# Padding the SBUF pools of a hybrid decoder step so that the operands of its large products begin at multiples of 256 bytes

## The chip, the core and the metric

The kernel runs on one core of a Trainium2 chip. The metric is the device time of one execution in microseconds, as the median of several. The profile is taken by the hardware profiler from one further execution.

## The reference

One inference step of a one-layer decoder, for a prompt of 2048 new tokens and for 8 sampled sequences of 8 new tokens with 8192 cached positions each. All data are float32. Cut to what matters:

```python
z = x @ w_in                                   # 1024 -> 3600 columns
fox = softmax(q k^T / 8 + L_i - L_j, causal) v # 8 heads of 64, forget gates as a bias
C, n, m, h = mlstm_scan(q, k, v, i, f)         # 4 heads of 128, matrix memory
mix = concat(fox, norm(h) * gate) @ w_o
x1  = layer_norm(ALPHA * x + mix)
hid = square(relu(x1 @ w1))                    # 1024 -> 4096
y   = layer_norm(ALPHA * x1 + hid @ w2)        # 4096 -> 1024
```

For the samples the attention also runs over pages of a key and value cache, which a page table points to.

## The kernel before

**Large products.** `mm3` (L152 to L155) makes each float32 product out of three single-pass products of a rounded high part and a low part: high by high (L153), low by high (L154), high by low (L155). `split_hi` on ScalarE (L145) writes the high part, `split_lo` on VectorE (L148) the low one. In `T.matmul(out, a, b)` the program loads `a` as the stationary operand and streams `b` past it. In the groups of the profile the streamed (moving) operand comes first: `ph<-x1h,wh 128*128 128x512` stands for a product into `ph` that streams 512 columns of `x1h` past 128 columns of `wh`. Each moving row of 512 float32 is 2048 contiguous bytes of a partition, and each stationary operand of 128 columns is 512 bytes.

**Stages.** Block A (`block_a`, called for four blocks of tokens) computes the input projection into PSUM tiles `pm`, with 256, 272 or 320 moving columns, and feeds the mLSTM recurrence (`m_block`, `m_sample`). Phase B (`phase_b`) does the prompt's attention, head by head: scores `pS` from `ks` and `qh`/`ql`, softmax, transposes `pt` of `S` into `PT`, and `po` from `vn` and `PT`. Phase O (`phase_o`) is the output projection `pw` from `wh`/`wl`, `woh`/`wol` and `mh`/`ml`, with the first layer norm. Phase C (`phase_c`) is the MLP: `ph` from `x1h`/`x1l` and the pieces `wh`/`wl` of w1, squared relu into `hh`/`hl`, and `py` from these and w2, added into `y`. In its last block 576 tokens are streamed as two pieces of 288 columns. The attention of the samples (`sample_attention`) is a generator that `tick` and `attend` advance in between: it gathers cache pages into `kT` and `vt` by indirect transfers and computes `sQ`, `sT` and `sO` in plain float32.

**Order.** The code gives a priority order; a planner at compile time lays out each engine's queue from it and inserts the waits. [...] Transfers are issued from the SP queue, and the gathers from GpSimd (POOL).

**SBUF.** Tiles are taken from pools. Left of the middle stand `cst` (L58) and then `pa` for block A, `pb` for phase B, or `pc` followed by `po` or `ph` for phases O and C. On the right stand `ps` (L85) for the samples, and below it `pm` or `pcw`, `pk`, `py`, `pob` and `px`. A pool's tiles follow one another in the order of their first use, each rounded to 32 bytes. A pool opened where an older one was reuses its bytes, and the first instruction on a new tile waits until the tiles that stood there are done with (`reuse_waits="tile"`). The constants `jp`, `ident`, `nhalf` and `gbias` make `cst` 1120 bytes long, so that what follows it does not begin at a multiple of 256.

The tiles that hold operands: `xn`, `wra`, `whi`, `wlo`, `xh0`, `xl0`, `xh1`, `xl1`, and `kT`, in `pa`; `kn`, `qn`, `qh`, `vn`, `ql`, `nl`, `ks`, `S`, `PT` in `pb`; `wh`, `wl` in `pc`; `mh`, `ml` in `po`; `hh`, `hl` in `ph`; `woh`, `wol` in `pob`; `x1h`, `x1l` in `px`; `wr`, `xr` in `pcw`; `PTs`, `vt` and `S` in `ps`.

Of the kernel before, what the change touches and what calls it, by code (L numbers as in the profile page):

```python
# [10 lines left out]
F32 = mybir.dt.float32  # L11
# [41 lines left out]
def body(ctx, tc, I, O, stages):  # L53
    nc = tc.nc
    V, A, G, T, SY = nc.vector, nc.scalar, nc.gpsimd, nc.tensor, nc.sync


    cst = ctx.enter_context(tc.tile_pool(name="cst", bufs=1))  # L58
# [20 lines left out]
    nhalf = cst.tile([128, 8], F32, name="nhalf")  # L79
    V.memset(nhalf, -0.5)  # L80
    gbias = cst.tile([128, 16], F32, name="gbias")


    es_s = ExitStack()
    ps_ = es_s.enter_context(tc.tile_pool(name="ps", bufs=1, side="right", reuse_waits="tile"))  # L85
# [101 lines left out]
    pa = es_a.enter_context(tc.tile_pool(name="pa", bufs=1, reuse_waits="tile"))  # L187
# [29 lines left out]
    V.memset(rm8.rearrange("p (c t) -> p c t", t=8)[:, :, 0], 0.0)  # L217
    Lend = pa.tile([8, 1], F32, name="Lend")
    mend = pa.tile([4, 1], F32, name="mend")

    head = [0, None]

# [595 lines left out]
    for bi in range(4):  # L818
        g = block_a(bi)
# [21 lines left out]
    def phase_b():  # L841
        es = ExitStack()
        pb = es.enter_context(tc.tile_pool(name="pb", bufs=1, reuse_waits="tile"))
# [94 lines left out]

        def values(z, g, sc):

            for i, (st, mx) in enumerate(sc):
                qt = 2 * g + i
                n = (qt + 1) * 128
                lp = pb.tile([128, 4], F32, name="lp", bufs=6)
                for k, sp in enumerate(st):
                    w = min(512, n - k * 512)
                    last["ACT"] = A.activation(sp[:, :w], sp[:, :w], AF.Exp, bias=mx[:, 7:8], accum_out=lp[:, k:k + 1])
                V.tensor_reduce(z["ls"][:, qt:qt + 1], lp[:, :len(st)], axis=AX.X, op=OP.add)

            po = ppb.tile([128, 256], F32, name="po", bufs=1)  # L950
            nk = 2 * g + 2
            for k0 in range(0, nk, 4):
                PT = pb.tile([128, 4, 256], F32, name="PT", bufs=4)
                for i in range(2):
                    kk = min(4, 2 * g + i + 1 - k0)
                    if kk <= 0:
                        continue
                    pt = ppb.tile([128, 4, 128], F32, name="pt", bufs=3)
                    for k in range(kk):
                        T.transpose(pt[:, k], sc[i][0][k0 // 4][:, k * 128:(k + 1) * 128], ident)  # L960
                    dst = PT[:, :kk, i * 128:i * 128 + 128]
                    if i == 0 or (k0 // 4) % 2 != 0:
                        A.copy(dst, pt[:, :kk])
                    else:
                        V.tensor_copy(dst, pt[:, :kk])
                for k in range(k0, min(k0 + 4, nk)):
                    q0 = 128 if k == nk - 1 else 0
                    c = (k % 2) * 64
                    last["PE"] = T.matmul(po[c:c + 64, q0:], z["vn"][:, k], PT[:, k - k0, q0:],
                                          start=(k < 2), stop=(k >= nk - 2), skip_group_check=True)  # L970
                tick(0.45 * min(4, nk - k0))
            if g % 4 == 0:
                z["ot"] = pb.tile([64, 1024], F32, name="ot", bufs=2)
            od = z["ot"][:, (g % 4) * 256:(g % 4) * 256 + 256]
            A.copy(od, po[0:64])
            q0 = 128 if g == 0 else 0
            V.tensor_tensor(od[:, q0:], od[:, q0:], po[64:128, q0:], op=OP.add)
            if g % 4 == 3:
                finish(z, g // 4)
# [23 lines left out]
        queries(Z[0], 0)  # L1003
        Z[0].update(head(0))
        dmask = masks[0]
        V.memset(dmask, 0.0)
        G.affine_select(dmask, dmask, pattern=[[-1, 128]], compare_op=OP.is_ge, fill=NEG, base=0, channel_multiplier=1)
        keys(Z[0], 0, kn)
# [2 lines left out]
        for n in range(len(units) + LA):  # L1011
# [4 lines left out]
            if n < len(units):  # L1016
                h, g = units[n]
# [11 lines left out]
            if n >= LA:  # L1029
                h, g = units[n - LA]  # L1030
# [71 lines left out]
    def phase_o(halves):  # L1102
        C["py"] = es_c.enter_context(tc.tile_pool(name="py", bufs=1, side="right", reuse_waits="tile"))
        C["pc"] = pc = es_c.enter_context(tc.tile_pool(name="pc", bufs=1, reuse_waits="tile"))
        es, es_b, es_x = ExitStack(), ExitStack(), ExitStack()
        po_ = es.enter_context(tc.tile_pool(name="po", bufs=1, reuse_waits="tile"))
        pob = es_b.enter_context(tc.tile_pool(name="pob", bufs=1, side="right", reuse_waits="tile"))
        ppo = es.enter_context(tc.tile_pool(name="ppo", bufs=1, space=PSUM, reuse_waits="tile"))

        def mix(t, eng):  # L1110
            mr = landing().rearrange("p (k c) -> p k c", k=8)
            SY.dma_start(mr, dmv[:, :, t * 128:(t + 1) * 128])
            mh = po_.tile([128, 8, 128], F32R, name="mh", bufs=2)
            ml = po_.tile([128, 8, 128], F32R, name="ml", bufs=2)
            split_hi(mh, mr)
            split_lo(ml, mr, mh, eng)
            return mh, ml

        vx["more"] = lambda: pob.tile([128, 1024], F32, name="vx", bufs=2)
        wh, wl = [[], []], [[], []]  # L1120

        def weights(hf):
            for q in range(4):
                r = halves.pop(0) if halves else half_wo(hf, q)
                if hf == 0:
                    h, l = piece(None, r)
                    if q == 0:
                        V.memset(pc.tile([128, 512], F32, name="hq", bufs=1)[:, 0:1], 0.0)
                else:
                    h = pob.tile([128, 2, 512], F32R, name="woh", bufs=4)  # L1130
                    l = pob.tile([128, 2, 512], F32R, name="wol", bufs=4)
                    split_hi(h, r)
                    split_lo(l, r, h)
                wh[hf] += [h[:, 0], h[:, 1]]
                wl[hf] += [l[:, 0], l[:, 1]]

        m, xs = {}, {}

        def begin(t):
            xs[t] = row()  # L1140
            SY.dma_start(xs[t], x_of(t))

        def unit(t, hf):
            s = slice(hf * 512, (hf + 1) * 512)
            ps = ppo.tile([128, 512], F32, name="pw", bufs=4)
            for k in range(8):
                mm3(ps, m[t][0][:, k], m[t][1][:, k], wh[hf][k], wl[hf][k], k == 0, k == 7)
            V.scalar_tensor_tensor(xs[t][:, s], xs[t][:, s], ALPHA, ps, op0=OP.mult, op1=OP.add)
            tick(5.1)

        def end(t):
            layer_norm(xs[t], 128, *gb, pc, "1")
            SY.dma_start(dx1[t * 128:(t + 1) * 128], xs[t])

        m[0] = mix(0, None)
        weights(0)
        m[1] = mix(1, None)
        begin(0)
        begin(1)
        unit(0, 0)  # L1160
        weights(1)
        unit(1, 0)
        gb = [bcast(I[f"ln1_{x}"], 0, D, f"{x}1", pcw, tag="wr", bufs=4) for x in "gb"]
        unit(0, 1)
        m[2] = mix(2, G)
        end(0)
        unit(1, 1)
        end(1)
        for t in range(2, 14):
            if t == 13:  # L1170
                vx["more"] = None
            m[t + 1] = mix(t + 1, G)
            begin(t)
            unit(t, 0)
            unit(t, 1)
            end(t)

        m[15] = mix(15, G)
        begin(14)
        begin(15)  # L1180
        nx = [x1_load(0), x1_load(1)]
        unit(14, 1)
        take_back()
        unit(15, 1)
        es_b.close()
        C["px"] = es_c.enter_context(tc.tile_pool(name="px", bufs=1, side="right", reuse_waits="tile"))
        ppx = es_x.enter_context(tc.tile_pool(name="ppx", bufs=1, space=PSUM, side="right", reuse_waits="tile"))
        px_of = lambda: ppx.tile([128, 4, 128], F32, name="px", bufs=2)
        x1_turn(0, 0, nx[0], px_of)
        nx.append(x1_load(2))  # L1190
        unit(14, 0)
        x1_turn(1, 1, nx[1], px_of)
        nx.append(x1_load(3))
        end(14)
        unit(15, 0)
        x1_turn(2, 2, nx[2], px_of)
        x1_turn(3, 3, nx[3], px_of)
        C["w1"] = w1_pieces(0)
        end(15)
        es_x.close()  # L1200
        es.close()
# [129 lines left out]
def sample_attention(tc, I, O, ps_, pps, cst, ident, dnl, dR, dmix, dqb, vx, kx, pa):  # L1331
# [46 lines left out]
    G.affine_select(tri, tri, pattern=[[-1, 128]], compare_op=OP.is_gt, fill=0.0, base=0, channel_multiplier=1)  # L1378
    V.memset(tri[64:128, 0:64], 0.0)
    onesr = ps_.tile([128, 1], F32, name="onesr")  # L1380
    V.memset(onesr, 1.0)
    LG = []
    for g in range(4):
# [2 lines left out]
    for g in range(4):  # L1386
        yield 1
        lv = LG[g].rearrange("p (t h) -> p t h", h=8)
        ri = pa.tile([128, 8, 129], F32, name="ri", tag="kT", bufs=1)
        V.memset(ri[:, :, 128], 0.0)  # L1390
        for h in range(8):
# [349 lines left out]
```

## Time and profile before

| | |
|---|---|
| median of 3 runs | 3387.81 us (3377.21 to 3388.4) |
| the profiled execution, its own time | 3392.21 us |
| its span, first to last instruction | 3390.5 us |
| mean granted TensorE clock | 0.985 |
| block A and the recurrence | to about 920 us |
| phase B | about 925 to 1370 us |
| phase O | about 1370 to 1600 us |
| phase C | about 1600 us to the end |

In the profile, PE is TensorE's matmuls and PEld its loads of stationary operands, DVE is VectorE, ACT ScalarE, POOL GpSimd. A group's row reads: line, engine, operation, output and inputs, stationary shape, moving shape, count, then busy microseconds, mean nanoseconds of one, and the idle time just before them with what ended it. A row of the timeline reads: start in microseconds, duration, engine, line, operation. Matmuls overlap, so that the time of one is read from start to start. A row of the waits gives the total, the number and the longest. In a row of stretches the columns are the stretch, its length, busy time of each engine with the number of instructions, granted clock, share of the DMA engines and GB/s.

### The profile page before, as it was taken

How to read it: one execution, taken by the hardware profiler on the slowest of the kernel's cores; microseconds unless marked ns; L12 is line 12 of the kernel's file. 1: busy time of each engine (PE TensorE's matmuls, PEld its weight loads, DVE VectorE, ACT ScalarE, POOL GpSimd, SP SyncE). 2: the span in 40 equal slices, each digit the busy share in tenths (PEclk: the TensorE clock that was granted, in tenths of full speed). 3: DMA queues.
4: the chain of work that ended last, by engine and by line, in shares of the span. 5: the costliest groups of instructions: out<-in, count | busy, mean ns of one | idle time of the engine just before them, and what ended most of it. 6: DMA issues, size and time to landing. Idle time of an engine off the chain costs nothing.

```text
span 3390.5 us, 58224 instructions
## 1 busy us (share of the span) xinstructions
PE 3263.4 (96%) x22065; PEld 2642.0 (78%) x22065; DVE 1884.5 (56%) x4774; ACT 1361.9 (40%) x2795; POOL 870.8 (26%) x925
## 2 busy tenths in 40 slices
PE   8999998999889999999999999999999999999998
PEld 8998998888756667676777777777776777888886
DVE  6847474464388887434444455445554445644545
ACT  4333343333278888313332333233333423433332
POOL 0131242323322222475223324323252110100000
PEclk9999999999999999999999999999999999999999
DMA  5575766766662322687777768667588444432221
GB/s 180 156 217 187 223 216 231 244 225 218 204 167 83 92 84 52 238 289 243 283 239 241 246 231 292 249 215 273 208 291 278 171 167 147 162 122 81 87 75 66
DMA packets 316001, 650.48 MB, mean 192 GB/s; under 512 B 61001, under 2 KB 175049, under 8 KB 314825
## 3 DMA queue, kind: packets, MB, share of 16 engines
q1 hardware_dynamic: 239032, 367.55, 35.4%
q0 software_dynamic: 74304, 270.57, 22.1%
q10 hardware_dynamic: 2384, 8.65, 0.7%
q8 instruction: 174, 2.85, 0.4%
q14 instruction: 107, 0.87, 0.1%
HBM read 593.82 MB, written 52.83 MB: 191 GB/s over the span
## 4 chain that ended last, share of the span: by engine, by line
PE 48%; DMA 3%; DVE 2%; issue 1%; ACT 1%; POOL 1%; another core or an unknown queue 0%; SPq 0%; POOLq 0%; ACTq 0%; DVEq 0%
PE py L153 7%; PE py L155 7%; PE py L154 7%; PE ph L153 7%; PE ph L155 7%; PE ph L154 7%; PE sO L1598 3%; PE sQ L1486 2%; DMA wr<-w 2%; PE sT L1555 1%; DVE wl L148 1%; PE pw L154 0%; PE pw L155 0%; PE pw L153 0%
## 5 line engine op out<-in xcount | busy, mean ns | idle before, releaser
L1292 DVE TENSOR_TENSOR y<-y,py 128x512 f32<-128x512 f32 (+1 forms) x476 | 324.1, 685 | 420.9 <-PE py L155 337.0
L145 ACT ACTIVATE wh<-wr 128x1024 fp32r<-128x1024 f32 x268 | 278.0, 1058 | 548.3 <-PE py L155 228.0
L153 PE MATMUL ph<-x1h,wh 128*128 128x512 f32 (+1 forms) x1280 | 458.4, 358 | 4.0 <-ACT wh L145 3.1
L154 PE MATMUL ph<-x1l,wh 128*128 128x512 f32 (+1 forms) x1280 | 456.7, 357 | 0.2 <-issue 0.2
L155 PE MATMUL ph<-x1h,wl 128*128 128x512 f32 (+1 forms) x1280 | 455.5, 357 | 0.9 <-issue 0.8
L153 PE MATMUL py<-wh,hh 128*128 128x512 f32 (+1 forms) x1088 | 438.4, 404 | 8.5 <-DVE y L1290 4.8
L1463 POOL DMA_INDIRECT kT<-cache_k,idxK x256 | 261.6, 1022 | 671.5 <-PE sQ L1486 610.3
L154 PE MATMUL py<-wl,hh 128*128 128x512 f32 (+1 forms) x1088 | 432.2, 397 | 0.6 <-DVE wl L148 0.6
L155 PE MATMUL py<-wh,hl 128*128 128x512 f32 (+1 forms) x1088 | 431.7, 397 | 0.0
L148 DVE TENSOR_TENSOR wl<-wr,wh 128x1024 fp32r<-128x1024 f32 x268 | 338.8, 1269 | 160.0 <-PE ph L155 47.1
L153 PE MATMUL pm<-xh,whi 128*128 128x256 f32 (+1 forms) x1024 | 301.9, 295 | 0.7 <-issue 0.4
L154 PE MATMUL pm<-xl,whi 128*128 128x256 f32 (+1 forms) x1024 | 297.9, 291 | 2.4 <-issue 2.3
L155 PE MATMUL pm<-xh,wlo 128*128 128x256 f32 (+1 forms) x1024 | 296.9, 290 | 2.8 <-issue 2.7
L153 PEld LDWEIGHTS ph<-x1h,wh 128*128 128x128 f32 x1280 | 241.4, 189 | 50.4 <-issue 8.9
L154 PEld LDWEIGHTS ph<-x1l,wh 128*128 128x128 f32 x1280 | 241.3, 189 | 38.9 <-issue 2.7
L155 PEld LDWEIGHTS ph<-x1h,wl 128*128 128x128 f32 x1280 | 241.2, 188 | 39.0 <-issue 2.1
L153 PEld LDWEIGHTS py<-wh,hh 128*128 128x128 f32 (+1 forms) x1088 | 202.0, 186 | 70.5 <-issue 16.3
L153 PE MATMUL pm<-whi,xh 128*128 128x256 f32 (+2 forms) x816 | 238.6, 293 | 9.9 <-ACT whi L145 8.5
L155 PEld LDWEIGHTS py<-wh,hl 128*128 128x128 f32 (+1 forms) x1088 | 202.2, 186 | 53.2 <-issue 2.5
L1574 POOL DMA_INDIRECT vt<-cache_v,idxV x158 | 159.9, 1012 | 314.8 <-PE sO L1598 240.7
L154 PEld LDWEIGHTS py<-wl,hh 128*128 128x128 f32 (+1 forms) x1088 | 202.4, 186 | 45.2 <-issue 1.6
L154 PE MATMUL pm<-wlo,xh 128*128 128x256 f32 (+2 forms) x816 | 233.9, 287 | 0.6 <-DVE wlo L148 0.6
(342 smaller groups left out, 6549.6 us busy)
## 6 DMA issues: line engine op xcount, KB each, us to landing
wr<-w SPq DMA_DIRECT2D x256, 512.0 KB
wra<-w_in SPq DMA_DIRECT2D x104, 512.0 KB
Rb<-dR SPq DMA_DIRECT2D x128, 128.0 KB
xn<-xp_t SPq DMA_DIRECT2D x16, 512.0 KB
kn<-k_prompt SPq DMA_DIRECT2D x64, 128.0 KB
qn<-dq SPq DMA_DIRECT2D x128, 64.0 KB
wr<-w_o SPq DMA_DIRECT2D x16, 512.0 KB
xr<-dmix SPq DMA_DIRECT2D x16, 512.0 KB
```

The lines of the kernel that those rows point to most:

```text
L145: last["ACT"] = A.activation(dst, src, AF.Copy, scale=scale)
L148: r = (eng or V).tensor_tensor(dst, src, hi.bitcast(F32), op=OP.subtract)
L153: T.matmul(ps, wh, xh, start=first, stop=False)
L154: T.matmul(ps, wh, xl, start=False, stop=False)
L155: last["PE"] = T.matmul(ps, wl, xh, start=False, stop=stop)
L1292: V.tensor_tensor(y, y, ps, op=OP.add)
L1463: G.indirect_dma_start(out=piece(n), out_offset=None, in_=ck, in_offset=IO(ap=idxK[:, b, j // 2, j % 2:j % 2 + 1], axis=0))
L1486: r = T.matmul(pq[h4 * 32:h4 * 32 + 32, hg].rearrange("p (k c) -> p k c", k=2), z["qb"][:, hd], kv, start=(db == 0), stop=(db == 1), skip_ ...
L1555: T.transpose(p[:, f], z["U"][u][:, hg, f].rearrange("p k t -> p (k t)"), ident)
L1574: G.indirect_dma_start(out=vt.rearrange("p f c -> p (f c)"), out_offset=None, in_=cv, in_offset=IO(ap=idxV[:, b, (kt % 4) * 4 + kt // 4, f ...
L1598: after_ = T.matmul(po[r:r + 32], z["PT"][:, hg, 2 * f + g, pg].rearrange("p h q -> p (h q)"), vts[f][:, g, hg * 256:(hg + 1) * 256], star ...
```

## The change

Seven small tiles, each with a memset of its first column, are put into the pools between the tiles that are there. Nothing else is altered; no tile that existed changes its size, and no existing instruction is added, removed or moved in the code. The pads are of 32 bytes a partition at the end of `cst`, 192 in `pa` ahead of `xn`, 64 in `pb` behind `dmask`, `ls` and `ks`, ahead of the score tiles, 64 in `pb` ahead of `PT`, 128 in `pc` behind the layer norm's small tiles, 192 in `ps`, and 128 in `pa` ahead of `kT`.

```diff
     gbias = cst.tile([128, 16], F32, name="gbias")
+    pads = []
+
+    def pad(pool, n):
+        pads.append(n)
+        V.memset(pool.tile([128, n // 4], F32, name=f"pad_{len(pads)}x")[:, 0:1], 0.0)
+
+    pad(cst, 32)
...
     mend = pa.tile([4, 1], F32, name="mend")
+    pad(pa, 192)
...
         def values(z, g, sc):
+            if z["h"] == 0 and g == 0:
+                pad(pb, 64)
             for i, (st, mx) in enumerate(sc):
...
         dmask = masks[0]
+        pad(pb, 64)
         V.memset(dmask, 0.0)
...
         weights(0)
+        pad(pc, 128)
         m[1] = mix(1, None)
...
     onesr = ps_.tile([128, 1], F32, name="onesr")
+    V.memset(ps_.tile([128, 48], F32, name="padS")[:, 0:1], 0.0)
     V.memset(onesr, 1.0)
...
         lv = LG[g].rearrange("p (t h) -> p t h", h=8)
+        if g == 0:
+            V.memset(pa.tile([128, 32], F32, name="pad2")[:, 0:1], 0.0)
         ri = pa.tile([128, 8, 129], F32, name="ri", tag="kT", bufs=1)
```

## The prediction

> **What bounds the kernel now.** I read the page's first two parts, then the groups of TensorE instructions with shapes kept apart, then single stretches of the timeline for the time from one matmul start to the next, then TensorE's waits.
>
> ```profile
> span 3390.5 us, 58224 instructions
> PE 3263.4 (96%) x22065; PEld 2642.0 (78%) x22065; DVE 1884.5 (56%) x4774; ACT 1361.9 (40%) x2795; POOL 870.8 (26%) x925
> PEclk9999999999999999999999999999999999999999
> ```
>
> TensorE covers 96% of the span in nearly every slice, at a granted clock of nine tenths or more; the next engine is at 56%. Its busy time is no measure of one matmul, since neighbours overlap; the step from start to start is. The waits are small beside it: 127 us of idle time in all, the three largest kinds being
>
> ```profile
> PE pt L960 <- ACT S L947: 13.1, 4, 11.4
> PE sO L1598 <- DMA vt<-cache_v,idxV: 12.7, 4, 7.1
> PE pm L153 <- ACT whi L145: 8.5, 1, 8.5
> ```
>
> So the kernel is bound by how fast the large products follow one another, and a nanosecond off each is worth what it is multiplied by. The groups give the counts (L154 and L155 repeat those of L153, L922 those of L921):
>
> ```profile
> L153 PE MATMUL py<-wh,hh 128*128 128x512 f32 x1024 | 413.3, 404 | 8.5 <-DVE y L1290 4.8 <-DVE y L1292 1.8 <-issue 1.8
> L153 PE MATMUL ph<-x1h,wh 128*128 128x512 f32 x768 | 307.6, 401 | 4.0 <-ACT wh L145 3.1 <-ACT x1h L145 0.5 <-issue 0.3
> L153 PE MATMUL pm<-xh,whi 128*128 128x256 f32 x896 | 261.7, 292 | 0.7 <-issue 0.4
> L153 PE MATMUL pm<-whi,xh 128*128 128x256 f32 x640 | 187.2, 293 | 1.5 <-issue 0.8 <-ACT qi L478 0.5
> L153 PE MATMUL ph<-x1h,wh 128*128 128x288 f32 x512 | 150.8, 295 | 0.0
> L921 PE MATMUL pS<-ks,qh 128*128 128x512 f32 x224 | 101.9, 456 | 0.4 <-ACT qh L145 0.2
> L153 PE MATMUL pw<-wh,mh 128*128 128x512 f32 x128 | 52.5, 411 | 2.4 <-ACT wh L145 2.4
> L153 PE MATMUL pw<-woh,mh 128*128 128x512 f32 x128 | 51.6, 404 | 2.6 <-ACT woh L145 2.6
> L153 PE MATMUL pm<-xh,whi 128*128 128x320 f32 x128 | 40.2, 314 | 0.0
> L153 PE MATMUL py<-wh,hh 128*64 128x512 f32 x64 | 25.1, 392 | 0.0
> ```
>
> With 512 moving columns: py 3(1024 + 64) = 3264, ph 3 x 768 = 2304, pw 3(128 + 128) = 768, pS 2 x 224 = 448, together 6784. With 288: 3 x 512 = 1536. In block A, 256 columns: 3(896 + 640) = 4608; 320: 384. Smaller shapes (272, 384, and 256 elsewhere) add some 800.
>
> **Where the operands begin now.** No row shows an address; these follow from the order and the sizes of the tiles, `cst` beginning 128 bytes past a multiple of 256. Within 256 bytes, moving / stationary: pm 32 / 32; pS 224 / 224; pw 224 or 192 / 96; ph 192 / 224, the second half of a 288 pair 64 / 224; py 224 / 96. None is at 0. Afterwards all are at 0, but for slices inside a tile (the second 288 half lands at 128). The change does what it says, and both ends of SBUF still have room, since the pads take a few hundred bytes a partition.
>
> **What a start costs, from the timeline.** The two 288 halves use the same weights in the same order and differ only in where the moving rows begin; first the half at 192, then the half at 64, each from the first product of an accumulation to 24 products later:
>
> ```profile
> 3022.52 0.29 PE L153 MATMUL ph<-x1h,wh 128*128 128x288 f32 x1
> ...
> 3025.71 0.30 PE L153 MATMUL ph<-x1h,wh 128*128 128x288 f32 x1
> 3052.37 0.30 PE L153 MATMUL ph<-x1h,wh 128*128 128x288 f32 x1
> ...
> 3055.53 0.40 PE L153 MATMUL py<-wh,hh 128*128 128x512 f32 x1
> ```
>
> 3.19 us and 3.16 us, 132.9 and 131.7 ns each: 1.3 ns (0.03 us over 24; the rounding of the two ends allows 0.5 to 2). A row of 1152 bytes from 192 touches six blocks of 256 bytes, from 64 only five. So I read 1.3 ns as the price of one more block touched. It is a reading: the blocks were not isolated. The other lengths:
>
> ```profile
> 1661.54 0.40 PE L155 MATMUL ph<-x1h,wl 128*128 128x512 f32 x1
> ...
> 1664.34 0.39 PE L155 MATMUL ph<-x1h,wl 128*128 128x512 f32 x1
> 3357.11 0.40 PE L153 MATMUL py<-wh,hh 128*128 128x512 f32 x1
> ...
> 3359.91 0.40 PE L153 MATMUL py<-wh,hh 128*128 128x512 f32 x1
> 99.76 0.28 PE L154 MATMUL pm<-wlo,xh 128*128 128x256 f32 x1
> ...
> 100.96 0.28 PE L155 MATMUL pm<-whi,xl 128*128 128x256 f32 x1
> 3371.12 0.39 PE L153 MATMUL py<-wh,hh 128*64 128x512 f32 x1
> ...
> 3373.87 0.40 PE L153 MATMUL py<-wh,hh 128*64 128x512 f32 x1
> 1392.97 0.63 PE L153 MATMUL pw<-woh,mh 128*128 128x512 f32 x1
> ...
> 1395.11 0.63 PE L155 MATMUL pw<-woh,ml 128*128 128x512 f32 x1
> ...
> 1390.00:1395.00 5.00, 3.54 (x9) 2.56 (x10) 3.94 (x4) 3.52 (x4) 0.43 (x1) 0.75 1.06 378
> ```
>
> ph and py with 512 columns: 2.80 us for 12, 233.3 ns each, although one starts at 192 and 32 bytes from its weights' position and the other at 224 and 128 bytes from it. pm with 256: 1.20 us for 10, 120 ns. py with 64 stationary columns: 2.75 us for 12, 229.2 ns. Just after a stall, in a stretch whose granted clock (third number from the end) is 0.75 in the mean, 2.14 us for 5, 428 ns. I take that for half speed; the same 512 columns would then cost 214 ns at full speed. So at full clock a 512 product carries some 19 ns that the slow clock does not show.
>
> **The change part by part.** (1) The moving operand. A 512 row is 2048 bytes: nine blocks from 192 or 224, eight from 0. One block for 6784 products, for half of the 1536 (192 goes to 0, while the half from 64 goes to 128 and stays at five), and for the 256s, the 320s and most small shapes, where five becomes four or six five: some 13,050 products x 1.3 ns = 17 us. Bounds: zero, since the two 512 rows do not tell 192 from 224; and the whole surplus, 19 ns x 6784 + about 13 ns x 7000 (120 against the 107 that 256 columns take at 214 for 512) = 220 us.
>
> (2) The stationary operand. 128 columns are 512 bytes, three blocks now and two afterwards. No row shows this alone. The nearest is the 64-column py, which is two blocks and half the load: 233.3 - 229.2 = 4.1 ns, so between 0 and 4.1. The load runs beside the product before it, so I take half of the moving price, 0.65 ns x 14,130 products = 9 us.
>
> (3) Seven new memsets of one column on VectorE, by the smallest memset there is:
>
> ```profile
> L210 DVE MEMSET qs<- 128x1 f32 x2 | 0.1, 59 | 0.0
> ```
>
> 7 x 59 ns = 0.4 us on an engine that is idle 44% of the time, hidden by the products; uncovered it would be 0.4 us. Each may wait until what stood at its place is free. In phases B and O VectorE's queue stands behind it: the masks and the score reductions in B, and in O the low halves of mix(1), with TensorE behind those. But their neighbours in the same bytes (ks, mh) wait for the same tenants, so I take 0; the row that bounds it is the one stall of 11.4 us at pt.
>
> (4) Moved tiles. A pool shifts by up to 352 bytes, so a few tiles overlap other old tenants, and the compile-time order may shift a little. No row prices it; I take 0, between minus and plus the largest waits, 8 to 13 us.
>
> (5) Transfers also land at multiples of 256. TensorE waits 12.7 us for the gathers; nothing says how much of it would go, so it counts 0, within 0 to 12.7. [...]
>
> Sum: -17 - 9 = -26 us. The profiled execution took 3392.2 us, 1.7 more than its span, so it would take 3366; it lies 4.4 above the median of 3387.8, so the forecast for the median is **3362**.
>
> **Rivals.** *The long row's surplus goes.* 256 columns pay 13 ns over the slow-clock rate and 512 pay 19. All 512s start in the last quarter of a block, the pm products in the first. If that start causes the extra 6 to 7 ns, 6784 x 6.6 = 45 us go: 3343, and more if the proportional part goes too. For it: the surplus vanishes at half clock, as a supply limit would. Against: length alone may make it. [...]
>
> *Nothing changes.* The surplus is the weight load's, whatever the addresses, and the 0.03 us is rounding or the halves' order: 3388. For it: ph and py agree at 233.3 with different starts. [...]
>
> *Slower: both streams at one place.* In the slower 288 half the moving row begins 32 bytes from the weights' position, in the faster one 160 away, and afterwards all pairs begin at the same position. If closeness is what 1.3 ns buys, and equal starts cost twice that, the py, ph and pw products, 3264 + 2304 + 768 and the 1536, pay 2.6 ns: 7872 x 2.6 = 20 us, 3408. It decides once it exceeds the 26 us of the sum or the sum is void. Against: pm is already at 32 / 32, and ph and py, 32 and 128 bytes apart, agree.
>
> **How the numbers follow.** Forecast 0.36, long row 0.26, nothing 0.16, slower 0.22. Faster or slower here means by over 0.5%, 17 us, about what a measurement of this kernel tells from no change. The forecast lies 26 us down with an error of some 15, so 0.25 of its 0.36 is faster; with all but a little of the long row, 0.50. Same: the rest of the forecast and the nothing case, 0.27. Slower: 0.23. The range goes up to 3410, the slower case, and down to 3275, half of the 220 us bound. The likeliest case alone has 3345 to 3380.
>
> **What would show it.** The step of 512 products, 233.3 now: about 231 by the forecast, 227 or less by the long row, 233 by nothing, over 235 by the slower one. The step of 256 products, 120 now, should fall to 118 to 119. Both 288 halves should come out alike. The forecast is wrong if these steps stand while the span moves (then it is order or waits: look at pt, sO and pm), or if 512 falls below 225.

## The result and the profile after

| | before | after |
|---|---|---|
| median | 3387.07 us (5 runs, 3377.21 to 3388.4) | 3354.03 us (5 runs, 3350.77 to 3360.61) |
| ratio | | 0.9911, 95% interval 0.9895 to 0.9927 |
| span of the profiled execution | 3390.5 us | 3352.3 us |

The change makes the kernel 33 us faster, 0.9%; the forecast was 3362 and 26 us. The page after, its first part and the granted clock:

```profile
span 3352.3 us, 58232 instructions
PE 3225.8 (96%) x22065; PEld 2635.4 (79%) x22065; DVE 1890.9 (56%) x4781; ACT 1364.1 (41%) x2795; POOL 877.3 (26%) x925
PEclk9999999999989999999999999999999999999999
```

The span lost 38.2 us and TensorE's busy time 37.6 (3263.4 to 3225.8); its idle time stayed, 127.1 to 126.5 us. So the products took less time, and the waits did not change in sum. VectorE has the seven memsets more. TensorE's waits after:

```profile
PE sO L1614 <- DMA vt<-cache_v,idxV: 27.0, 11, 6.1
PE pt L971 <- ACT S L958: 13.6, 6, 10.9
PE pm L161 <- ACT whi L153: 9.0, 1, 9.0
```

The waits of `sO` for `vt` rose from 12.7 to 27.0 us, and with those for the other gathered tiles (`kT`, `xr`, `vx`) the waits for gathers rose from 14.1 to 41.5 us; pt and pm stand as they were. Against it, the waits that the view puts down to "issue", in which the engine waited for nothing that the profile shows, fell from 18.5 us to none. Why the two changed places is not shown. (Lines are shifted by the change: L161 to L163 are the three products of `mm3`.)

Where the time went, by stretches; the columns are the stretch, its length, busy time and count of PE, PEld, DVE, ACT, POOL, granted clock, DMA share, GB/s. Before:

```profile
0.00:920.00 920.00, 871.63 (x7451) 818.89 (x7451) 534.69 (x1575) 327.49 (x698) 232.35 (x263) 0.98 0.66 208
920.00:1370.00 450.00, 422.36 (x2880) 293.28 (x2880) 347.22 (x1376) 363.67 (x1026) 111.42 (x171) 0.97 0.36 99
1600.00:3390.00 1790.00, 1747.87 (x10410) 1364.18 (x10408) 903.43 (x1592) 613.37 (x990) 390.13 (x384) 0.99 0.58 197
```

After:

```profile
0.00:920.00 920.00, 868.50 (x7451) 817.06 (x7451) 537.64 (x1582) 330.56 (x699) 235.91 (x264) 0.98 0.66 208
920.00:1370.00 450.00, 422.21 (x2881) 293.06 (x2881) 348.69 (x1379) 365.64 (x1027) 111.78 (x171) 0.98 0.34 99
1600.00:3352.00 1752.00, 1714.11 (x10363) 1358.29 (x10359) 903.86 (x1590) 612.50 (x989) 393.27 (x384) 0.99 0.58 201
```

Block A and phase B got through the same number of products in nearly the same time: from the first `pm` to the first `pS` it is 918.4 us before and 915.5 after, from there to the first `pw` 445.0 and 444.3. The gain is in phase C: from the first `ph` to the last `py` product it is 1766.5 us before and 1731.2 after, 35 us less. (The last stretch above is 38 us shorter because it has a fixed start, and phase C began 3 us earlier.) The timeline after, from the first of each pair of rows to the second: twelve `ph` steps, twelve `py` steps, sixteen `pm` steps, and the two halves of a 288 pair with 24 steps each:

```profile
1613.21 0.39 PE L162 MATMUL ph<-x1l,wh 128*128 128x512 f32 x1
...
1615.93 0.39 PE L162 MATMUL ph<-x1l,wh 128*128 128x512 f32 x1
1659.40 0.39 PE L161 MATMUL py<-wh,hh 128*128 128x512 f32 x1
...
1662.12 0.39 PE L161 MATMUL py<-wh,hh 128*128 128x512 f32 x1
99.07 0.28 PE L162 MATMUL pm<-wlo,xh 128*128 128x256 f32 x1
...
100.99 0.28 PE L163 MATMUL pm<-whi,xl 128*128 128x256 f32 x1
2936.85 0.29 PE L161 MATMUL ph<-x1h,wh 128*128 128x288 f32 x1
...
2940.01 0.29 PE L161 MATMUL ph<-x1h,wh 128*128 128x288 f32 x1
...
2943.21 0.40 PE L161 MATMUL py<-wh,hh 128*128 128x512 f32 x1
```

`ph` and `py` with 512 columns: 2.72 us for 12, 226.7 ns where 233.3 stood. `pm`: 1.92 for 16, 120.0, as before. The 288 halves: 131.7 and 133.3 ns; they did not come out alike. Taken over all steps between neighbours of one kind and length that no stall breaks (means, ns):

| products | before | after |
|---|---|---|
| ph, 512 columns (2304) | 233.1 | 227.7 |
| py, 512, 128 stationary columns (3072) | 232.7 | 228.6 |
| py, 512, 64 stationary columns (192) | 229.3 | 228.5 |
| pw, 512 (768) | 233.1 | 228.1 |
| pm, 256 (4608) | 119.7 | 119.7 |
| pm, 320 (384) | 146.6 | 146.6 |
| ph, 288, first / second half (1536) | 133.3 / 131.9 | 131.3 / 133.6 |

2304 x 5.4 + 3072 x 4.1 + 192 x 0.8 + 768 x 5.0 = 29 us, against 33 between the medians. In phase O the 3.8 us of pw did not arrive: first pw to first ph is 238.1 us before and 238.2 after, and TensorE there waits 3.9 us for a gathered page of the value cache, which it did not before. In phase C the steps explain 25 of 35 us. Shorter stalls give 4 (idle time 42.1 to 37.9 us), and fewer products at half clock some 2: between those two products the profile grants half clock for 15 us before and for 10 after. The remaining 4 us or so I did not find in the one pair of profiles.

### The profile page after: what moved, and what is told of

The parts are those of the page before. It is cut to its first block, busy times and chain, and to the rows that moved or that the text cites. A ratio compares the mean times of both kernels' runs of the same rounds, so it can differ in the third digit from the quotient of the medians.

```text
span 3352.3 us, 58232 instructions
## 1 busy us (share of the span) xinstructions
PE 3225.8 (96%) x22065; PEld 2635.4 (79%) x22065; DVE 1890.9 (56%) x4781; ACT 1364.1 (41%) x2795; POOL 877.3 (26%) x925
## 4 chain that ended last, share of the span: by engine, by line
PE 47%; DMA 4%; DVE 1%; POOL 1%; issue 1%; ACT 1%; SPq 0%; ACTq 0%; POOLq 0%; DVEq 0%
PE py L161 7%; PE py L162 7%; PE py L163 7%; PE ph L161 6%; PE ph L163 6%; PE ph L162 6%; PE sO L1614 3%; PE sQ L1502 2%; DMA wr<-w 2%; DMA vt<-cache_v,idxV 1%; PE sT L1571 1%; DMA kT<-cache_k,idxK 1%; DVE wl L156 0%; DMA vx<-cache_v,idxV 0%; PE pw L162 0%
## 5 line engine op out<-in xcount | busy, mean ns | idle before, releaser
L161 PE MATMUL ph<-x1h,wh 128*128 128x512 f32 (+1 forms) x1280 | 455.1, 356 | 4.3 <-ACT wh L153 3.8
L163 PE MATMUL ph<-x1h,wl 128*128 128x512 f32 (+1 forms) x1280 | 451.4, 353 | 0.2 <-DVE wl L156 0.2
L161 PE MATMUL py<-wh,hh 128*128 128x512 f32 (+1 forms) x1088 | 432.6, 398 | 3.6 <-DVE y L1303 3.6
L163 PE MATMUL py<-wh,hl 128*128 128x512 f32 (+1 forms) x1088 | 425.8, 392 | 0.0
L161 PE MATMUL pm<-xh,whi 128*128 128x256 f32 (+1 forms) x1024 | 302.4, 295 | 0.0
L163 PE MATMUL pm<-xh,wlo 128*128 128x256 f32 (+1 forms) x1024 | 297.0, 290 | 0.0
L161 PEld LDWEIGHTS ph<-x1h,wh 128*128 128x128 f32 x1280 | 241.3, 189 | 45.7 <-issue 7.0
L163 PEld LDWEIGHTS ph<-x1h,wl 128*128 128x128 f32 x1280 | 241.2, 188 | 35.5 <-issue 2.1
L161 PEld LDWEIGHTS py<-wh,hh 128*128 128x128 f32 (+1 forms) x1088 | 200.9, 185 | 60.6 <-issue 14.0
L161 PE MATMUL pm<-whi,xh 128*128 128x256 f32 (+2 forms) x816 | 237.6, 292 | 9.2 <-ACT whi L153 9.0
L163 PEld LDWEIGHTS py<-wh,hl 128*128 128x128 f32 (+1 forms) x1088 | 200.9, 185 | 49.5 <-issue 2.5
```

Source lines behind the costliest of these rows:

```text
L161: T.matmul(ps, wh, xh, start=first, stop=False)
L163: last["PE"] = T.matmul(ps, wl, xh, start=False, stop=stop)
```

## The experiments

What the profile after leaves open is why 512 columns gained 5 ns and 256 none, and whether multiples of 256 matter at all. In what follows the *distance* of a product is the start of its moving operand minus that of its stationary operand, modulo 256 bytes. Before, it was 224 for ph (96 for the second half of a 288 pair), 128 for py, 128 and 96 for pw, 0 for pm and pS; after, it is 0 for all of these but the second 288 half, which has 128.

**One side of SBUF alone.** The left pools keep their pads, the right side does not move: x1h at 192, wh at 0, so ph has distance 192, py 0.

```diff
-    V.memset(ps_.tile([128, 48], F32, name="padS")[:, 0:1], 0.0)
```

> The 192-byte pad in ps is left out, so what stands right of the middle (x1h and x1l of ph, woh and wol of the second half of pw) begins at 192 again, and everything on the left stays at 0. Theory (the start of the moving row decides): ph with 512 columns goes back to a step of 233 ns, py and the first half of pw stay at 227, and the time lies about 2304 + 384 products x 5.5 ns = 15 us above the changed kernel, near 3369. Rival (the start of the stationary operand decides, which is 0 in all of them here): ph stays at 227 and the time near 3354. Rival (both must begin at the same place): as the theory, ph 233.

Measured 3375.09 us against 3385.61, ratio 0.9973 (0.9958 to 0.9988). The timeline, twelve steps of ph and of py:

```profile
1612.01 0.39 PE L161 MATMUL ph<-x1h,wh 128*128 128x512 f32 x1
...
1614.81 0.39 PE L161 MATMUL ph<-x1h,wh 128*128 128x512 f32 x1
1657.84 0.39 PE L161 MATMUL py<-wh,hh 128*128 128x512 f32 x1
...
1660.58 0.39 PE L161 MATMUL py<-wh,hh 128*128 128x512 f32 x1
```

ph takes 2.80 us, 233.3 ns each, though its stationary operand is at a multiple of 256; py 2.74, 228.3 (229.5 in the mean of all its steps). Only the products with both operands at one place got faster. The time lies 6 us above the 3369 that was expected, which these steps do not explain in full.

**The other side alone.** Without the 32 bytes in `cst` the left pools stand at 224 and the right side at 0: ph has its *moving* operand at 0 and its stationary one at 224.

```diff
-    pad(cst, 32)
```

> The 32-byte pad in cst is left out, so everything on the left begins at 224 and the right stays at 0: ph streams from 0 past weights at 224, py streams from 224 past weights at 224. Theory (moving start decides): ph 227 ns, py 233 ns, time near 3369. Rival (stationary start decides): ph and py both 233, time near 3387. Rival (the two must begin at the same place within 256 bytes): py 227 and ph 233, time near 3369 as well, but with ph and py exchanged.

Measured 3371.33, ratio 0.9949 (0.9933 to 0.9966). Twelve steps of ph and of py:

```profile
1615.10 0.39 PE L160 MATMUL ph<-x1h,wh 128*128 128x512 f32 x1
...
1617.90 0.39 PE L160 MATMUL ph<-x1h,wh 128*128 128x512 f32 x1
1660.23 0.40 PE L160 MATMUL py<-wh,hh 128*128 128x512 f32 x1
...
1662.96 0.39 PE L160 MATMUL py<-wh,hh 128*128 128x512 f32 x1
```

2.80 and 2.73 us for 12. Mean steps: ph (moving at 0, stationary at 224) 233.3 ns, py (both at 224) 229.1, pw from wh (both at 224) 228.6, pw from woh (0 and 224 again) 233.3. A moving operand at 0 gains nothing by itself, and both at 224 gain as much as both at 0. My theory that the moving operand's start decides fell with this.

**Everything at 128, everything at 64.** All operands at one place that is not a multiple of 256 (the pads in `cst` and `ps` are 160 and 64 bytes, or 96 and 128):

```diff
-    pad(cst, 32)
+    pad(cst, 160)
-    V.memset(ps_.tile([128, 48], F32, name="padS")[:, 0:1], 0.0)
+    V.memset(ps_.tile([128, 16], F32, name="padS")[:, 0:1], 0.0)
```

> The pads of cst and ps are sized so that every operand begins at 128 in place of 0. Theory with a period of 256 bytes: ph and py at 233 ns, time near 3387. With a period of 128 or less, or if only the equal place of both counts: 227 ns and near 3354.

> As before, with every operand at 64. Theory with a period of 256 or 128 bytes: 233 ns and near 3387. If a multiple of 64 is enough, or only the equal place of both counts: 227 ns and near 3354.

3364.41 (0.9932, 0.9915 to 0.9948) and 3359.44 (0.9919, 0.9902 to 0.9936). Both have the steps of the changed kernel, ph 227.7 ns, py 228.7 and 228.6; here ph at 128:

```profile
1619.77 0.39 PE L161 MATMUL ph<-x1h,wh 128*128 128x512 f32 x1
...
1622.49 0.39 PE L161 MATMUL ph<-x1h,wh 128*128 128x512 f32 x1
```

2.72 us for 12. The longer time of the first goes with its granted clock, 0.983 in the mean of its runs and 0.985 in those of the changed kernel: at 0.983 its two runs took 3361 and 3363 us, and the changed kernel's one run at 0.983 took 3361. For the step of these products the absolute place made no difference.

**Two pads in place of seven.** The kernel before, with nothing but these two; ph, py, pw and pS are then at 224 on both sides, pm stays at 32 on both.

```diff
         weights(0)
+        V.memset(pc.tile([128, 32], F32, name="padC")[:, 0:1], 0.0)
         m[1] = mix(1, None)
...
+    V.memset(ps_.tile([128, 56], F32, name="padS")[:, 0:1], 0.0)
     V.memset(onesr, 1.0)
```

> The kernel before with two pads only: 128 bytes in `pc` behind the layer norm's small tiles and 224 bytes in `ps`. Moving and stationary operand of ph, py, pw and pS then both begin at 224 within 256 bytes, pm stays at 32 / 32; none begins at a multiple of 256. Theory (the two operands of a product must begin at the same place within 256 bytes; which place does not matter): steps of the 512-column products 227 to 229 ns, time 3354 within 5 us, the whole gain of the change. Rival (places count too, by transfers that land at multiples of 256 or by rows that touch fewer blocks): steps of 228 to 231, time 3360 to 3370. If multiples of 256 were what counts: 233 and 3387.

Measured 3365.20 (3357.16 to 3374.18, the clock of its runs between 0.982 and 0.987), 0.9923 (0.9889 to 0.9957), an interval that holds the changed kernel's 0.9911. The steps are the same (ph 227.6, py 228.7, pw 228.1):

```profile
1660.33 0.39 PE L153 MATMUL py<-wh,hh 128*128 128x512 f32 x1
...
1663.05 0.39 PE L153 MATMUL py<-wh,hh 128*128 128x512 f32 x1
```

12 steps in 2.72 us, with no operand of a large product at a multiple of 256. The time does not settle it as well as the steps do: 3365 lies in the range of the rival (3360 to 3370), and at a granted clock of 0.984 this kernel took 3365 twice, where the changed kernel took 3352 to 3362 in five runs. So the two pads give the steps of the seven; that they give the whole gain in time is not shown.

**One pad taken away.** The changed kernel without the pad in `pc`. That pad stands behind wh and ahead of mh and hh, so it is mh and hh, the stationary operands of pw and py, that move to 128, and not wh, as the expectation has it; the distances are those it names, 128 for py and pw, 0 for ph.

```diff
         weights(0)
-        pad(pc, 128)
```

> The changed kernel without its 128-byte pad in `pc`: `wh` and `wl` of phases O and C then begin at 128, `hh`, `hl`, `mh`, `ml` and the right side stay at 0. Here ph streams x1h (0) past wh's slices, py and pw have one operand at 0 and the other at 128. Theory: py and pw, 3264 + 768 products, go back to 233 ns (+4 to 5 each, 16 to 20 us), and ph stays at 228 if its two operands are still at one place: 3370 to 3374. Rival (the moving place alone counts): nothing changes, 3354. Rival (the pad's order effects, not the places, carried the gain): 3380 or more with steps of 228.

Measured 3372.54, 0.9956 (0.9934 to 0.9978). ph and py:

```profile
1613.21 0.39 PE L163 MATMUL ph<-x1h,wl 128*128 128x512 f32 x1
...
1615.93 0.39 PE L163 MATMUL ph<-x1h,wl 128*128 128x512 f32 x1
2485.29 0.39 PE L161 MATMUL py<-wh,hh 128*128 128x512 f32 x1
...
2488.09 0.39 PE L161 MATMUL py<-wh,hh 128*128 128x512 f32 x1
```

ph 2.72 us for 12, py 2.80; the means are 228.1 and 232.6, pw 232.7. 3072 x 4.0 + 768 x 4.6 = 16 us, and the time is 18 above the changed kernel's, 15 by the two ratios. So the loss sits where the distance is, in the same program with the same other pads.

**Block A at distance 128.** The changed kernel with a further pad ahead of the first xh0.

```diff
             w = 256 if i else 320
+            if bi == 0 and i == 0:
+                V.memset(pa.tile([128, 32], F32, name="padX")[:, 0:1], 0.0)
```

> The changed kernel with a further pad of 128 bytes in `pa` ahead of the first `xh0`, so that in block A the two operands of every pm product begin 128 bytes apart (0 and 128); phases O and C are untouched. Theory A (distance costs any product, and block A gained nothing only because its operands stood at one place before): the 256-column step rises from 119.7 by what the 288-column pair shows, about 2 ns, on some 5000 products: 10 us, 3364. Theory B (only long rows feel the distance): 119.7 stays, 3354. Rival (the loss for 512 columns is a fixed cost of the load): +5 ns, 25 us, 3379.

Measured 3352.26, 0.9888 (0.9838 to 0.9938), and none of the three theories: the pm step fell, from 119.7 to 118.7 ns. For 256 columns the same place on both sides is not the best one. (One ns on 4608 products is 5 us; four runs from 3344 to 3368 us cannot tell it from nothing.)

**Products alone.** The computation is left out; groups of 24 products of one length and distance follow one another, accumulated in one PSUM tile a group:

```python
def run(n, d, s=lambda k: 0, m=128, cnt=24):
    ...
    for k in range(cnt):
        so = s(k) // 4 + (k % 8) * 128
        mo = (d(k) if callable(d) else d) // 4 + (k % 8) * 512
        T.matmul(p[:m, :n], sta[:, so:so + m], mov[:, mo:mo + n], start=(k == 0), stop=(k == cnt - 1))
```

> The whole computation is left out; in its place 1920 single-pass float32 products run back to back, 24 in a group, and their steps are read from the trace. Groups: 512, 448, 384, 320, 288, 256, 192 and 128 moving columns, each with the moving operand 0, 32, 64 to 224 bytes past the place of the stationary one; 512 columns with 4, 8, 16, 48 and 240; the stationary or the moving operand alternating between 0 and 128, both alternating together, and both alternating in opposition; 64 stationary columns at 0 and 128. Theory (own operands must begin at one place): 512 columns 227 to 229 at 0 and 233 at every other distance; with both alternating together 228, in opposition 233. Rival (a product's row against the weights loaded beside it for the next product): together 233, in opposition 228, and with the stationary one alternating the step of a product at one place is the slow one. Rival (the program around it makes the difference, not the places): all groups of a length alike. For lengths: if the surplus goes with the row's bytes, 448 gains about 4, 256 about 2; if only rows of 2048 bytes feel it, 448 and below are flat.

The timeline has the 22 inner products of a group in one row: start, then the time from the first start to the last end. The rows are 512 columns at distances 0, 32, 64, 128, then 256 columns at 0, 128, 192:

```profile
33.34 5.15 PE L80 MATMUL q<-mov,sta 128*128 128x512 f32 x22
38.79 5.29 PE L80 MATMUL q<-mov,sta 128*128 128x512 f32 x22
44.39 5.20 PE L80 MATMUL q<-mov,sta 128*128 128x512 f32 x22
55.51 5.29 PE L80 MATMUL q<-mov,sta 128*128 128x512 f32 x22
204.15 2.79 PE L80 MATMUL q<-mov,sta 128*128 128x256 f32 x22
215.54 2.78 PE L80 MATMUL q<-mov,sta 128*128 128x256 f32 x22
221.21 2.66 PE L80 MATMUL q<-mov,sta 128*128 128x256 f32 x22
```

5.15 less one product's 0.39, over 21 steps, is 226.7 ns; 5.29 is 233.3; 2.66 is 0.13 below the row at distance 0, 6 ns a step. All groups, mean step in ns from start to start; each cell is a single group of 24:

| columns | 0 | 32 | 64 | 96 | 128 | 160 | 192 | 224 |
|---|---|---|---|---|---|---|---|---|
| 512 | 226.7 | 233.3 | 228.9 | 233.9 | 233.3 | 234.0 | 233.3 | 233.0 |
| 448 | 202.5 | 206.4 | 199.9 | 205.2 | 203.9 | 206.5 | 202.5 | 204.4 |
| 384 | 173.4 | 173.4 | 173.3 | 176.7 | 176.3 | 176.7 | 174.6 | 174.3 |
| 320 | 146.5 | 146.7 | 146.7 | 146.6 | 146.5 | 146.8 | 146.5 | 146.7 |
| 288 | 132.1 | 133.5 | 132.3 | 131.6 | 133.3 | 132.7 | 133.4 | 133.1 |
| 256 | 119.5 | 117.7 | 117.8 | 119.5 | 118.8 | 117.4 | 113.5 | 118.1 |

192 and 128 columns take 111.5 to 111.9 at every distance. The distance alone makes the difference, with no program around it. My sentence "233 at every other distance" was wrong at 64, and of the smaller or further distances 48 gave 233.3 but 16 gave 231.8 and 240 gave 236.6. Neither guess on the lengths holds: each length has its own best distance, 0 for 512, 64 for 448, none for 320, 192 for 256. With 64 stationary columns in place of 128, 512 moving ones took 229.6 at distance 0 and 231.1 at 128, where 128 stationary columns took 226.7 and 233.3. The 288 row has the pair that the prediction read: 133.1 at 224 and 131.6 at 96 are the two halves before (133.3 and 131.9), 132.1 and 133.3 at 0 and 128 those after. With 512 columns and both operands alternating together between 0 and 128 the step was 228.3, in opposition 230.0, with the stationary one alone alternating 232.3, with the moving one 230.1: neither a product's own pair alone nor the moving row against the next product's load alone gives these four.

**The table used.** For block A it says 192. The 192-byte pad of `pa` moves from ahead of xn to ahead of the first xh0; xh is then at 0 and the weights at 64. Products that stream xh have distance 192, those that stream whi 64.

```diff
-    pad(pa, 192)
...
             w = 256 if i else 320
+            if bi == 0 and i == 0:
+                V.memset(pa.tile([128, 48], F32, name="padX")[:, 0:1], 0.0)
```

> The changed kernel with the 192-byte pad of `pa` moved from ahead of `xn` to ahead of the first `xh0`: in block A `xh`/`xl` begin at 0 and the weights at 64, so that a pm product that streams `xh` is 192 past its stationary operand (2688 products of 256 columns) and one that streams `whi`/`wlo` is 64 past it (2040 products). Phases B, O and C as in the changed kernel. Theory (a table of steps by length and distance, read from the run of products alone, holds inside the kernel too: 256 columns 113.5 ns at 192, 117.8 at 64, 119.5 at 0): the step of pm<-xh falls from 119.7 to 113.5, that of pm<-whi to 117.8; 2688 x 6.2 + 2040 x 1.9 = 20 us less than the changed kernel, 3330 to 3338 where that one gives 3354. Rival (the three products of mm3 mix two operands in a row, and the best distance of a lone run is lost): as at 128, 118 to 119 and 3350. Rival (block A's pace is set elsewhere): steps fall, the time stays at 3354.

With a pad of 64 bytes there, and the old one kept, the two distances change places:

> The changed kernel with a further pad of 64 bytes ahead of the first `xh0`: the two distances of block A are exchanged, 64 for the products that stream `xh`, 192 for those that stream `whi`. Theory (the table holds): pm<-xh 117.8, pm<-whi 113.5; 2688 x 1.9 + 2040 x 6.2 = 18 us less than the changed kernel, about 3336. Rival (the sign of the distance does not matter): both 113 to 118 alike in this kernel and in the one at 192. Rival (mixing spoils it): 118 to 119, 3350.

Beside them ran the changed kernel once more:

> The changed kernel itself, on the chip of the two runs beside it, as what they are measured against: 3354, ratio to the kernel before 0.990 to 0.992.

| kernel | median, us | ratio to before (3385.75) | pm from xh | pm from whi |
|---|---|---|---|---|
| changed, again | 3355.24 | 0.9908 (0.9889 to 0.9927) | 119.7 (at 0) | 119.7 (at 0) |
| xh 192 past the weights' place | 3342.41 | 0.9861 (0.9842 to 0.9881) | 114.9 (at 192) | 117.1 (at 64) |
| xh 64 past it | 3346.86 | 0.9880 (0.9860 to 0.9901) | 117.3 (at 64) | 114.9 (at 192) |

The step goes with the signed distance and not with the operand. Both times lie above what was expected (3330 to 3338, and about 3336), as the steps at 192 do (114.9 for 113.5). The timeline of the kernel with 192, sixteen steps that stream xh and thirty-two that stream whi:

```profile
57.12 0.28 PE L163 MATMUL pm<-xh,wlo 128*128 128x256 f32 x1
...
58.94 0.28 PE L161 MATMUL pm<-xh,whi 128*128 128x256 f32 x1
105.73 0.28 PE L163 MATMUL pm<-whi,xl 128*128 128x256 f32 x1
...
109.50 0.28 PE L162 MATMUL pm<-wlo,xh 128*128 128x256 f32 x1
```

1.82 us for 16, about 113.7 ns, and 3.77 for 32, 117.8. The mean at 192 is 114.9 since stretches of 113.4 and of 117.8 alternate. By the steps 2688 x 4.8 + 2040 x 2.6 = 18 us should go; 13 went between the medians. Runs of the two kernels with the same granted clock differ by 13 us (at 0.986, one run against two) and by 17 (at 0.984, three against three), so part of the gap may be clock. The wait for the gathers is another place where it may be, in the changed kernel run beside it and then in the kernel with 192:

```profile
PE sO L1614 <- DMA vt<-cache_v,idxV: 25.6, 11, 6.0
```

```profile
PE sO L1615 <- DMA vt<-cache_v,idxV: 30.8, 10, 8.8
```

5 us more, though the second profile also had the lower clock (0.982 against 0.986), so the two waits do not compare cleanly. The kernel with 192 has the lowest median of all kernels that ran with the computation in, 43 us under the kernel before.

**Finer steps.** Again the computation is left out.

> The whole computation is left out; in its place are groups of 24 products as in the run of products alone. First, 512 columns where after twelve products only the stationary operand, or only the moving one, changes its place (0 to 128, 0 to 32, 128 to 0, 0 to 64). If a product's own pair counts, the step changes from the first product with the new place on; if the load that runs beside it counts, one product earlier when the stationary one changes and not when the moving one does. Then 512 columns at distances in steps of 4 to 16 bytes around 0, 32 and 64, and 256 columns around 192: if the cost goes with blocks of 32 or 64 bytes it is flat inside one; if it is a matter of phase it slides. Then 256 columns with other strides from product to product (1024, 1280 and 4096 bytes moving, 512, 1024 and 1088 stationary): the table should hold at each (113.5 at 192) where the strides are multiples of 256, and not at 1088. Then both operands moved together by 32, 128 and 192: unchanged, 227 at distance 0 for 512 and 113.5 at 192 for 256. Then lengths near 256 and near 512 (240, 248, 264, 272, 480, 496, 504) at 0, 64, 128 and 192: if the best distance goes with the length, it moves by the bytes of the length; 264 and 272 tell how fast.

512 columns, distance: 4 bytes 236.0 (in the first run of products alone), 8 233.2, 12 229.9, 16 231.8, 20 240.0, 24 232.6, 28 230.1, 32 233.5. The inside of the groups at 0, 20 and 28:

```profile
101.78 5.15 PE L80 MATMUL q<-mov,sta 128*128 128x512 f32 x22
123.92 5.44 PE L80 MATMUL q<-mov,sta 128*128 128x512 f32 x22
135.25 5.22 PE L80 MATMUL q<-mov,sta 128*128 128x512 f32 x22
```

It is not flat inside a block of 32 or 64 bytes, and distances that are multiples of 16 bytes do not share a step either: 226.7 at 0, 231.8 at 16, 233.5 at 32.

In the trace of the run of products alone, the load of the next stationary operand starts 3 ns after a product of 512 columns and takes 188 ns, so it runs beside that product. When after twelve products at 0 the stationary operand moved to 128 or 32, the step of the product *before* the first new one rose already, to 232 and 235 ns from 226 or 227; with a move to 64 it did not (225). When the moving operand moved, the first new product was the first slow one (234, 236, 237). Both are what the expectation has for the load that runs beside a product, but for the move to 64. After a return to 0 it took 3 to 10 products until 227 stood again.

Strides of 1024, 1280, 2048 and 4096 bytes from one moving operand to the next made no difference (256 columns at 192: 117.8 ns); a stride of 1088 from one stationary operand to the next, with which the distance changes from product to product, gave 116.4 to 118.0 ns for 256 columns whatever the first distance. As for the lengths near 512 and 256, the best of the four distances tried was 192 for 496 (220.0; 223.0 at 0), 480 (216.0; 216.9 at 0) and 272 (123.5; 125.5 at 0), and 0 for 504 (227.4). Sixteen columns fewer than 512 are 64 bytes fewer, and the best distance moved by as much; but 480 does not follow that rule, so it is not shown that the best distance goes with the bytes of the length.

Further, 512 columns with both operands moved together by 192 gave 226.7, and by 32 and 128 they settled towards it. The lone 113.5 for 256 columns at 192 came back once, as 114.1; in the later groups at the same distance it was 117.8, also with the very strides of the first run. The same places thus allow two paces, and I do not know what chooses.

## Why the prediction was right, and where it was not

The number was near, 3362 against 3354, and that is luck: the steps behind it were mostly wrong. The forecast gave the 6784 products of 512 columns 13 of its 26 us, where the steps gained 29, and the shorter products the other 13, where the steps gained next to nothing.

**(1) The moving operand, 1.3 ns for each block of 256 bytes: failed.** "A row of 1152 bytes from 192 touches six blocks of 256 bytes, from 64 only five" explained a true difference by the wrong one of two properties. The 288 halves before stood also at distances 224 and 96, which the text names further on, in the slower rival, and that is what separates them. After the change both touch five blocks and differ more, 131.3 and 133.6. And with all operands at 224 a row of 512 still touches nine blocks, yet takes 227.6 ns. Measured, 6144 products of 512 columns (all but pS and the py with 64 stationary columns) gained 4 to 5.4 ns in place of 1.3, and the 4992 of 256 and 320 columns in block A gained nothing in place of 1.3: the distance of their operands was 0 before (32 / 32) and after.

**(2) The stationary operand, 9 us: failed.** With the stationary operand alone at 0, ph stays at 233.3 (the left side alone), and with all operands at 128, where 128 columns touch three blocks as before, it has the 227.7 of the changed kernel; no price of the start alone shows. The bound of 4.1 ns came from the py with 64 stationary columns. The run of products alone has such a product at 229.6 at distance 0, where one with 128 columns takes 226.7, so it was no measure of fewer blocks or a shorter load.

**(3) and (4) as forecast, (5) not.** The memsets cost nothing visible (VectorE 1884.5 to 1890.9 us at 56%), and order and waits changed nothing in sum (idle 127.1 to 126.5). The landing of transfers, taken at 0 within a gain of 12.7, did not shorten the waits for the gathers: they grew by 27 us, and only a fall elsewhere kept the sum.

**The rivals.** The *long row's surplus* had the size, "227 or less" for the 512 step, and the wrong cause: it blamed a start in the last quarter of a block, and with all operands at 224 the step is the same 227.6. That the surplus vanishes at half clock spoke for nothing: the 214 ns it is counted from are half of the step at half clock. The *slower* case asked the right question, where the two streams begin against each other, with the sign turned round: for 512 columns the equal start is the cheap one (226.7 ns for the products alone, 228.9 to 234.0 in the rest of the row). The row it was weighed against, pm at 32 / 32, was the key to why block A would gain nothing: its distance does not change. *Nothing changes* rested on ph and py agreeing at 233.3 with different starts; they agreed because 224 and 128 cost the same (233.0 and 233.3 for the products alone), and the cheap distance 0 was one that none of ph, py and pw had.

## What to carry to other kernels

Where TensorE is back to back with a fresh stationary operand for each product, as here, lay out the two operands by their distance modulo 256 bytes, not by an alignment. In these runs the good distances were 0 for rows of 512 float32 (226.7 ns alone, 233.3 at 128) and 192, or else 64, for rows of 256 (114.9 and 117.1 in the kernel, 119.7 at 0); find other lengths by a table like the one above, with more than one group to a cell, since 256 columns at 192 had two paces (113.4 and 117.8). By the steps, two pads did here what seven do (ph 227.6 and 227.7). When a pair of rows differs in two properties, a prediction that picks one should price the other too, before its sign is guessed.

## What was not expected of the hardware

- In the profile before, products of 512 columns in stretches with a granted clock of 0.50 follow one another every 426.7 ns (39 steps); the stretch that the prediction took for half speed is among them. Half of that, 213.3 ns, is an estimate of what the columns alone take at full clock. By that measure, scaled with the length, a product at its best distance takes 13 ns more with 512, 448, 384 and 320 columns (226.7 against 213.3, 199.9 against 186.7, 173.3 against 160.0, 146.6 against 133.3) and 7 more with 256 (113.5 against 106.7); with 240, 192 and 128 columns the step stands at about 112 ns whatever the length.
- The surplus above that depends on the distance in single elements: at 20 bytes a product took 240 ns, at 28 bytes 230, at 0 226.7.
- After a break the first ten or so products of 512 columns at distance 0 run slower: in the changed kernel the first four steps of an unbroken stretch of sixteen or more are 231 to 234 ns for ph and 231 to 235 for pw, and from the eleventh on they are 226.7. So a stage with many breaks gains less: py, whose unbroken stretches have nine steps in the mean, 228.6, ph, with twelve, 227.7. Before, at distances 224 and 128, the early and the late steps were alike (233.0 and 233.3 for ph). pS had distance 0 before and after and yet took 233.4 and 232.8; its stretches have at most four steps, so the breaks are enough to explain it, though no run has pS without them.
- In the profile before, 4376 of the 22065 loads of stationary operands start ahead of the matmul that stands before them, all of them among the small products sQ, sO and po. Among the large products there is none.
- What the mechanism is stays open. The switches of the stationary operand to 128 and 32 (232 and 235 ns one product early) show that the load beside a product takes part, and the alternating groups (228.3 together, 230.0 in opposition) that it is not the only partner.
